# Transposing k one chunk earlier, with its sums of squares on TensorE, and shorter stated waits behind two triangular solves

## The chip, the cores and the metric

The kernel runs on one core of a Trainium2 chip. Its measure is the time of one execution on the device, in microseconds (us). The engines are PE (matrix products), DVE (vector), ACT (activations), POOL (the second vector engine) and SP (which issues the DMAs spoken of here). Each engine takes its instructions in the order of the program.

## The reference, cut to what matters

The reference is a block with attention, pooling and a mixture of experts, followed by a second block of two layers. Only the second block's layers are changed. One of them projects the 512 tokens onto many columns and feeds three branches, whose outputs are gated and projected back. The branch that the change touches is a gated delta rule:

```
h = rms_norm_2(x, norm_g[layer])
cols = split_columns(h @ w_in[layer])
...
qkv = jax.nn.silu(centred_depthwise_conv(qkv, conv_w))
q, k, v = jnp.split(qkv, [GDN_QK_W, 2 * GDN_QK_W], axis=-1)
...
k = l2_normalize(k.reshape(b, l, GDN_HEADS, GDN_DK))
...
a_mat = beta[..., :, None] * jnp.einsum('nhcid,nhcjd->nhcij', k, k) * d_strict
...
sol = lax.linalg.triangular_solve(a_mat, rhs, left_side=True, lower=True, unit_diagonal=True)
...
_, o = lax.scan(step, s0, xs)
```

`l2_normalize` multiplies by the reciprocal root of the sum of squares over a head's 64 columns. The second branch is a latent attention (`mla_branch`), the third a recurrence (`rwkv7_branch`) that the kernel also evaluates in chunks with a triangular solve of its own.

## The kernel before, in words

The first block takes the first 838 us. Each layer of the second block then goes through the same stages, layer 0 from about 838 to 1395 us and layer 1 from there to the end.

The projection (`Project`) makes 27 chunks of 128 columns. A chunk is eight steps of three products `mm<-hh,wh`, `mm<-hl,wh`, `mm<-hh,wl`; three such products are called a triple here, so a chunk is 8 triples. The plan of chunks is: the decay inputs, the three of k, four of the gate, three of q, three of v, seven of the third branch's, two of the attention's latents, four of the gate. Behind a chunk of q, k or v, `qkv` (L1281) convolves it along the tokens with one ACT and four DVE instructions (L1289, L1293), applies silu with a tanh on ACT and a product on DVE (L1296, L1303), and puts a function `take` on a list, with the count of chunks after which `columns` (L1223) calls it. `take_k` (L1427) transposes k into the tile `kt` (PE L159, ACT L1432).

`Gdn` then works in this order: `gates` and `triangles` (decay factors); `keys` (L1500) squares `kt` on POOL, sums the squares on DVE, normalizes `kt` (L1515) and transposes it back into `kq`; `squares` (L1549, tiles `x<-kq`) makes the products of keys and multiplies them into the triangle `M`; `inverse` (L1608) sends `M` through DRAM (`mud`) into the tile `au`, one triangle to a partition, and `solve` (L1332) inverts blocks of 32 x 32 by 30 steps of two dependent DVE instructions each (`stmp<-au`, `au<-au,stmp`). The result goes through DRAM (`xud`) to the tile `XT`, is transposed by DVE (L1633, L1635) and completed to 64 x 64 by PE (`x<-XT,AO`, then `x<-LT,XT`, from `off_diagonal`). `chain` (L1646) carries the state over eight steps (`kp`, `pu`, `kp`) and ends in four output groups (`kp`, `pu` of 24 products each).

`Rwkv.prepare` (L1804) is the third branch's preparation: its products `mm<-w,rw`, `mm<-cst,lw`, `mm<-cst,sq` depend on one another through DVE; then come triangles (`x<-KR,BB`, `M`), the same kind of solve, and `mm<-XT,AO`, followed by its states. The attention `mla` (L2149) has products `mm<-mch,...`, `mm<-kT,qT`, `mm<-cst,e` and `mo`.

The order of PE is written by hand. Each stage is a generator; `yield x` says that the stage's next PE work should wait until x us of PE work, by the kernel's own count `pe_us`, has been issued from elsewhere. `braid` (L161) takes the first stream that is due, so the number sets how much other work stands between two pieces of a stage; it is no wait on the chip. Streams are woven as `first` (gates to inverse) with `project`, `second` (the chain) with `project`, then `project`, which goes on into `prepare`, with `others` (attention, then rows of the output projection), then `states` with `others`. A stage whose input is late holds PE, since everything behind it is queued. The other engines' orders come from a scheduler and are fixed too. The lines of the waits in question:

```
        yield 19
        for t in range(NT):
...
        yield 44
        while not self.decayed:
...
        yield 26
        yield from off_diagonal(net, lambda: self.pa.tile([128, 2, 512], F32, name="x2", bufs=1), self.AO, XP, LT, T, 24, fac)
...
                yield 50
                yield from off_diagonal(net, lambda: psum.tile([128, 1, 512], F32, name="mm", bufs=2), AO, XP, LT, T, 16, None)
```

Of the kernel before, what the change touches and what calls it, by code (L numbers as in the profile page):

```python
# [8 lines left out]
F32 = mybir.dt.float32  # L9
# [3 lines left out]
AF = mybir.ActivationFunctionType  # L13
ALU = mybir.AluOpType
AX = mybir.AxisListType
PSUM = bass.MemoryType.PSUM

S = 512
D = 1024
NT = 4  # L20
# [78 lines left out]
def tok(t):  # L99
    return slice(128 * t, 128 * t + 128)  # L100
# [1027 lines left out]
class Project:  # L1128
# [152 lines left out]
    def qkv(self, g, ms):  # L1281


        net, nc, tmp = self.net, self.net.nc, self.tmp
        cw = net.smalls.cw[:, self.l]
        for m in ms:
            ps = yield from self.columns()
            y = tmp.tile([128, S], F32, name="y", bufs=4)
            nc.scalar.activation(y, ps, AF.Copy, scale=cw[:, 2, m:m + 1])  # L1289
            for j in (0, 1, 3, 4):  # L1290
                d = j - 2
# [5 lines left out]
            if m < 3:  # L1297
                z = g.kq[:, m, :, 64:128]
# [5 lines left out]
            self.pend.append((self.count + 1, partial(self.take, g, m, y)))  # L1304

    def take(self, g, m, y):
        (g.take_q, g.take_k, g.take_v)[m // 3](self, m % 3, y)
        g.have.add(m)
# [72 lines left out]
class Gdn:  # L1381


    def __init__(self, net, ctx, a, l, ab):
        self.net, self.a, self.l = net, a, l
        tc, nc = net.tc, net.nc
        p = self.pool = ctx.enter_context(pool(tc, "gd"))
# [23 lines left out]
        m = self.midp = self.mid.enter_context(pool(tc, "gdm"))  # L1411
# [5 lines left out]
        self.kt = self.ta.tile([128, NT, 384], F32, name="kt", bufs=1)  # L1417

# [8 lines left out]
    def take_k(self, pj, m, z):  # L1427
        net, nc = self.net, self.net.nc
        ps = pj.psum.tile([128, 512], F32, name="tr", bufs=1)
        for t in range(NT):  # L1430
            net.transpose(ps[:, tok(t)], z[:, tok(t)], net.ident)
        nc.scalar.activation(self.kt[:, :, tok(m)], ps.rearrange("p (t c) -> p t c", t=NT), AF.Copy)  # L1432
# [67 lines left out]
    def keys(self):  # L1500

        net, nc, tmp, psum, kt = self.net, self.net.nc, self.ta, self.pa, self.kt
        while not self.have.issuperset((3, 4, 5)):
            yield 1
        ss = tmp.tile([128, NT, 6], F32, name="ss", bufs=1)
        for t in range(NT):
            sq = tmp.tile([128, 6, 64], F32, name="sq", bufs=1)
            kv = kt[:, t].rearrange("p (h d) -> p h d", d=64)
            nc.gpsimd.tensor_tensor(sq, kv, kv, op=ALU.mult)
            nc.vector.tensor_reduce(ss[:, t], sq, AX.X, ALU.add)  # L1510
        r = net.rstd(tmp, ss.rearrange("p t h -> p (t h)"), [128, 24], 1, 1e-6, "rk").rearrange("p (t h) -> p t h", t=NT)
        yield 19
# [95 lines left out]
    def inverse(self, mud, xud):  # L1608
# [14 lines left out]
        yield 44  # L1623
# [16 lines left out]
        yield 26  # L1640
# [108 lines left out]
class Rwkv:  # L1749
# [54 lines left out]
    def prepare(self, mud, xud):  # L1804
# [16 lines left out]
        with pool(tc, "rka", 1, "right") as tmp, pool(tc, "rks", 2, "right") as small, pool(tc, "rpa", 1, "right", PSUM) as psum:  # L1821
# [160 lines left out]
            def inverse():  # L1982
# [24 lines left out]
                yield 50  # L2007
# [531 lines left out]
```

## Time and profile before

| | |
|---|---|
| three runs | 1902.6, 1907.91 (median), 1915.12 us |
| profiled execution | 1903.25 us, span 1901.5 us |
| mean granted clock of PE | 0.930 of full speed |
| PE busy | 1653.5 us (87%), 14010 instructions |
| DVE busy | 1046.3 us (55%) |
| ACT, POOL busy | 583.7 us (31%), 558.4 us (29%) |

The span runs from the first to the last instruction of the profiled execution; 1.75 us of its time lie around it. Busy shares are means over stages with different limits: in one stage PE never pauses, in another it waits for a result from DVE or from DRAM. A wait is shown with the engine and line that ended it; "issue" is idle time that ended with nothing that the profile shows. A granted clock of 1.0 is 2.4 GHz, one near 0.5 is 1.2 GHz.

### The profile page before, as it was taken

To read this page: it belongs to the slowest core of one execution; us is meant where nothing else is said; L and a number is where in the kernel's file an instruction comes from. 1 tells how busy PE (TensorE), PEld (TensorE's weight loads), DVE (VectorE), ACT (ScalarE), POOL (GpSimd) and SP (SyncE) were. 2 spreads that over 40 slices of the span, in tenths; PEclk is the share of its full clock that TensorE was granted. 3 is DMA by queue.
4 is the path that set the end of the run, shared out by engine and by line. 5 is a ranking of instruction groups with operands and counts; after the bars stand their busy time and mean duration, and the time that the engine had idled before them with its cause. 6 is when DMAs were issued, how large, how long until landed. Compare 5 with 4: busy or idle time off the path is not lost.

```text
span 1901.5 us, 34119 instructions
## 1 busy us (share of the span) xinstructions
PE 1653.5 (87%) x14010; PEld 1100.7 (58%) x14010; DVE 1046.3 (55%) x2224; ACT 583.7 (31%) x1154; POOL 558.4 (29%) x559
## 2 busy tenths in 40 slices
PE   5999998999999999959978968777789799789776
PEld 3986584444444444438756755455577577545554
DVE  2435534344434333355895567836656875678456
ACT  4344432212121212144432124331344331244212
POOL 1113111000000000025651243454335721354443
PEclk8899998999999999979988989898889999989888
DMA  9934726999999999833424120123433441201332
GB/s 310 238 107 139 257 74 221 393 392 398 399 406 400 392 399 396 308 102 95 106 68 99 62 73 21 30 93 106 133 84 94 112 111 50 53 33 39 99 111 89
DMA packets 243219, 337.10 MB, mean 177 GB/s; under 512 B 92769, under 2 KB 166161, under 8 KB 226225
## 3 DMA queue, kind: packets, MB, share of 16 engines
q1 hardware_dynamic: 241152, 329.88, 50.3%
q10 hardware_dynamic: 1152, 3.22, 0.5%
q8 instruction: 112, 1.84, 0.4%
q0 software_dynamic: 752, 1.76, 0.3%
q14 instruction: 51, 0.41, 0.1%
HBM read 310.84 MB, written 23.99 MB: 176 GB/s over the span
## 4 chain that ended last, share of the span: by engine, by line
PE 25%; DVE 17%; DMA 5%; issue 4%; POOL 3%; ACT 2%; SPq 1%; DVEq 0%; POOLq 0%; ACTq 0%
PE mm L149 17%; DVE stmp L1342 2%; DVE au L1344 2%; PE mm L159 2%; PE tr L149 1%; PE x L149 1%; PE pu L149 1%; PE kp L149 1%; DMA w<-in_w_out_dram 1%; DMA au<-mud 1%; DVE nm L2233 1%; DVE y L1293 1%; PE mo L149 1%; DMA gate<-gated 1%; POOL w L2310 1%
## 5 line engine op out<-in xcount | busy, mean ns | idle before, releaser
L149 PE MATMUL gu<-w,XT 128*64 128x512 f32 x1024 | 225.8, 594 | 0.0
L149 PE MATMUL mm<-hh,wh 128*128 128x512 f32 (+1 forms) x464 | 203.9, 440 | 0.0
L149 PE MATMUL mm<-hh,wl 128*128 128x512 f32 (+1 forms) x464 | 188.4, 406 | 0.0
L149 PE MATMUL mm<-hl,wh 128*128 128x512 f32 (+1 forms) x464 | 188.1, 405 | 0.0
L928 POOL TENSOR_TENSOR yl<-y,yh 128x512 fp32r<-128x512 f32 x30 | 38.1, 1270 | 451.4 <-ACT yh L927 451.4
L149 PEld LDWEIGHTS gu<-w,XT 128*64 128x64 f32 x1024 | 72.1, 137 | 142.7 <-issue 136.2
L938 DVE TENSOR_TENSOR xres<-mm,xres 128x512 f32<-128x512 f32 x128 | 79.2, 681 | 90.7 <-PE mm L149 90.7
L149 PE MATMUL mm<-w,hT 128*64 128x512 f32 x512 | 113.4, 595 | 0.7 <-ACT hT L912 0.7
L149 PE MATMUL mm<-w,mh 128*128 128x512 f32 x256 | 92.9, 442 | 22.8 <-POOL w L2310 10.0
L149 PEld LDWEIGHTS mm<-hh,wh 128*128 128x128 f32 (+1 forms) x464 | 91.6, 198 | 26.6 <-issue 3.5
L149 PEld LDWEIGHTS mm<-hh,wl 128*128 128x128 f32 (+1 forms) x464 | 91.1, 196 | 21.0
L149 PEld LDWEIGHTS mm<-hl,wh 128*128 128x128 f32 (+1 forms) x464 | 91.8, 198 | 19.1 <-DVE hl L1162 0.2
L1214 ACT ACTIVATE wh<-w 128x1024 fp32r<-128x1024 f32 (+1 forms) x54 | 57.0, 1056 | 145.8 <-PE mm L149 105.9
L1216 POOL TENSOR_TENSOR wl<-w,wh 128x1024 fp32r<-128x1024 f32 (+1 forms) x28 | 69.4, 2478 | 110.0 <-ACT wh L1214 91.3
L149 PE MATMUL mm<-wh,hh 128*128 128x256 f32 x320 | 93.8, 293 | 2.2 <-ACT hh L357 2.2
L149 PE MATMUL mm<-wh,hl 128*128 128x256 f32 x320 | 91.0, 284 | 4.3 <-DVE hl L359 4.0
L2238 POOL TENSOR_SCALAR e<-e,rs 128x512 f32<-128x512 f32 x48 | 75.5, 1574 | 65.3 <-DVE rs L2237 59.8
L149 PE MATMUL mm<-wl,hh 128*128 128x256 f32 x320 | 90.6, 283 | 1.6 <-DVE wl L381 1.6
L149 PEld LDWEIGHTS mm<-w,hT 128*64 128x64 f32 x512 | 35.3, 137 | 66.6 <-issue 62.5
L149 PEld LDWEIGHTS mm<-w,mh 128*128 128x128 f32 x256 | 50.1, 206 | 41.1 <-POOL w L2310 12.5
L1342 DVE TENSOR_TENSOR stmp<-au 96x60 f32<-96x60 f32 (+29 forms) x120 | 64.5, 537 | 14.3 <-DMA au<-rmud 6.5
L872 ACT ACTIVATE X<-mm,ws 128x512 f32<-128x512 f32 x32 | 22.0, 688 | 151.4 <-DVE ws L869 128.1
(580 smaller groups left out, 3596.3 us busy)
## 6 DMA issues: line engine op xcount, KB each, us to landing
w<-in_w_gate_dram SPq DMA_DIRECT2D x64, 1024.0 KB, 13.2
w<-in_w_up_dram SPq DMA_DIRECT2D x64, 1024.0 KB, 13.4
w<-in_w_down_dram SPq DMA_DIRECT2D x64, 1024.0 KB, 10.0
w<-in_w_in_dram SPq DMA_DIRECT2D x52, 512.0 KB, 4.1
w<-in_w_ada_dram SPq DMA_DIRECT2D x24, 1024.0 KB, 8.5
w<-in_w_out_dram SPq DMA_DIRECT2D x16, 512.0 KB, 3.8
w<-in_w_in_dram SPq DMA_DIRECT2D x6, 1024.0 KB, 12.1
w<-in_w_out_dram SPq DMA_DIRECT2D x4, 1024.0 KB, 6.3
```

What stands on the lines that cost most here:

```text
L149: return self.nc.tensor.matmul(out, a, b, **kw)
L159: return self.nc.tensor.transpose(out, a, ident)
L872: nc.scalar.activation(X[:, 512 * i:512 * i + 512], ps, AF.Copy, scale=ws[:, 1:2])
L928: (nc.vector if last else nc.gpsimd).tensor_tensor(yl[:, hs], y, yh[:, hs].bitcast(F32), op=ALU.subtract)
L938: nc.vector.tensor_tensor(net.xres[:, t, hs], po, net.xres[:, t, hs], op=ALU.add)
L1214: nc.scalar.activation(h[:, :, :m], w[:, :, :m], AF.Copy)
L1216: eng.tensor_tensor(lo[:, :, :m], w[:, :, :m], h[:, :, :m].bitcast(F32), op=ALU.subtract)
L1293: nc.vector.scalar_tensor_tensor(y[:, lo:hi], ps[:, lo + d:hi + d], cw[:, j, m:m + 1], y[:, lo:hi], op0=ALU.mult, op1=ALU.add)
L1342: nc.vector.tensor_tensor(tv, au[:n, :, j + 1:, j:j + 1].to_broadcast(sh), au[:n, :, j:j + 1, 0:j].to_broadcast(sh), op=ALU.mult)
L1344: nc.vector.tensor_tensor(au[:n, :, j + 1:, 0:j], au[:n, :, j + 1:, 0:j], tv, op=ALU.add)
L2233: nc.vector.tensor_reduce(nm, ps, AX.X, ALU.max, negate=True)
L2238: nc.gpsimd.tensor_scalar(e, e, rs, None, op0=ALU.mult)
```

## The change

`qkv` makes, for a chunk of k, a second tile `sq` with the squares of the convolved k, by one ACT instruction more, and puts `take_k` on the list for the end of the next chunk in place of the one after that. `take_k` first multiplies the squares by a constant of 128 x 2 (`head`), four PE instructions `tr<-cst,sq`, which sums them over each head, copies the sums by DVE to a new tile `kss`, and then transposes as before. `keys` loses its four POOL squares and four DVE sums, and its stated wait goes from 19 to 8. Three more stated waits change: in `inverse` 44 to 34 and 26 to 20, in `Rwkv.prepare`'s `inverse` 50 to 42.

```diff
@@ -1301,10 +1301,15 @@
                 nc.scalar.activation(c8(y), z, AF.Square)
             else:
                 nc.vector.scalar_tensor_tensor(y, th, 1.0, y, op0=ALU.add, op1=ALU.mult)
-            self.pend.append((self.count + 1, partial(self.take, g, m, y)))
-
-    def take(self, g, m, y):
-        (g.take_q, g.take_k, g.take_v)[m // 3](self, m % 3, y)
+            if m // 3 == 1:
+                sq = tmp.tile([128, S], F32, name="sq", tag="y", bufs=4)
+                nc.scalar.activation(sq, y, AF.Square)
+                self.pend.append((self.count, partial(self.take, g, m, y, sq)))
+            else:
+                self.pend.append((self.count + 1, partial(self.take, g, m, y)))
+
+    def take(self, g, m, *y):
+        (g.take_q, g.take_k, g.take_v)[m // 3](self, m % 3, *y)
         g.have.add(m)
 
     def rw(self, rw):
@@ -1415,6 +1420,7 @@
         self.ta = self.sa.enter_context(pool(tc, "gda", 2))
         self.pa = self.sa.enter_context(pool(tc, "gpa", 1, "left", PSUM))
         self.kt = self.ta.tile([128, NT, 384], F32, name="kt", bufs=1)
+        self.kss = self.ta.tile([128, NT, 6], F32, name="kss", bufs=1)
 
 
     def take_q(self, pj, m, z):
@@ -1424,8 +1430,12 @@
             net.matmul(ps[:, 2 * t:2 * t + 2], z[:, tok(t)], net.const("head"), start=True, stop=True)
         nc.vector.tensor_copy(self.ssq[:, :, :, m], ps[:, :8].rearrange("p (t a) -> p t a", t=NT))
 
-    def take_k(self, pj, m, z):
+    def take_k(self, pj, m, z, sq):
         net, nc = self.net, self.net.nc
+        ps = self.pa.tile([128, 512], F32, name="tr", bufs=2)
+        for t in range(NT):
+            net.matmul(ps[:, 2 * t:2 * t + 2], sq[:, tok(t)], net.const("head"), start=True, stop=True)
+        nc.vector.tensor_copy(self.kss[:, :, 2 * m:2 * m + 2], ps[:, :8].rearrange("p (t a) -> p t a", t=NT))
         ps = pj.psum.tile([128, 512], F32, name="tr", bufs=1)
         for t in range(NT):
             net.transpose(ps[:, tok(t)], z[:, tok(t)], net.ident)
@@ -1502,14 +1512,8 @@
         net, nc, tmp, psum, kt = self.net, self.net.nc, self.ta, self.pa, self.kt
         while not self.have.issuperset((3, 4, 5)):
             yield 1
-        ss = tmp.tile([128, NT, 6], F32, name="ss", bufs=1)
-        for t in range(NT):
-            sq = tmp.tile([128, 6, 64], F32, name="sq", bufs=1)
-            kv = kt[:, t].rearrange("p (h d) -> p h d", d=64)
-            nc.gpsimd.tensor_tensor(sq, kv, kv, op=ALU.mult)
-            nc.vector.tensor_reduce(ss[:, t], sq, AX.X, ALU.add)
-        r = net.rstd(tmp, ss.rearrange("p t h -> p (t h)"), [128, 24], 1, 1e-6, "rk").rearrange("p (t h) -> p t h", t=NT)
-        yield 19
+        r = net.rstd(tmp, self.kss.rearrange("p t h -> p (t h)"), [128, 24], 1, 1e-6, "rk").rearrange("p (t h) -> p t h", t=NT)
+        yield 8
         for t in range(NT):
             kv = kt[:, t].rearrange("p (h d) -> p h d", d=64)
             nc.vector.tensor_tensor(kv, kv, r[:, t, :, None].to_broadcast([128, 6, 64]), op=ALU.mult)
@@ -1620,7 +1624,7 @@
         nc.sync.dma_start(xud, au)
         for z in range(2):
             nc.sync.dma_start(XP[half(z)], xud[48 * z:48 * z + 24].rearrange("u b i c -> (b i) u c"))
-        yield 44
+        yield 34
         while not self.decayed:
             yield 1
         LT = self.LT = self.pool.tile([128, 2, 24, 64], F32, name="LT", tag="ld")
@@ -1637,7 +1641,7 @@
         nc.vector.tensor_scalar(fac, bu[:, 0], -1.0, None, op0=ALU.mult)
         for b in (0, 2):
             nc.vector.memset(fac[quarter(b)], -1.0)
-        yield 26
+        yield 20
         yield from off_diagonal(net, lambda: self.pa.tile([128, 2, 512], F32, name="x2", bufs=1), self.AO, XP, LT, T, 24, fac)
 
         yield 2
@@ -2004,7 +2008,7 @@
                     nc.vector.transpose(LT[quarter(b), 0, :, c0:c0 + 32], XP[quarter(b)])
                     if b % 2:
                         nc.vector.transpose(XP[quarter(b)], LT[quarter(b), 1, :, c0:c0 + 32])
-                yield 50
+                yield 42
                 yield from off_diagonal(net, lambda: psum.tile([128, 1, 512], F32, name="mm", bufs=2), AO, XP, LT, T, 16, None)
 
             def rest():
```

Lines from `qkv` on stand five to ten lines lower in the changed kernel. Counted in triples since the layer's first transposes of `mch`, both layers alike, PE's order has k's transposes behind triples 24, 32 and 40 before and 16, 24 and 32 now; the last product of `squares` behind 82 before and 57 now; `x<-XT,AO` behind 174 before and 133 now. Between the last of `squares` and `x<-XT,AO` stand 92 triples before and 76 now. The chain's eight steps and four output groups began behind 175 and ran on into `prepare`, which begins behind 208; now they lie between 140 and 188. Between the last product of the third branch's triangles and its `mm<-XT,AO` stand 18 products `mm<-kT,qT`, 60 `mm<-cst,e`, 48 `mo`, 4 `mm<-wv,mch` and one `mm<-t,cst` before, and 13, 52, 56, none and none now. From a layer's start to that `mm<-XT,AO` the order now holds 2 `mm<-kT,qT`, 8 `mm<-cst,e` and 16 `mo` more than before, which stood behind it.

PE at the start of `Rwkv.prepare` in layer 0, before. The products with `w`, `lw` and `sq` are `prepare`'s; `kp` and `pu` are the chain's, and the products of 24 begin its output groups:

```order
L149 MATMUL mm<-rw,w_7715 128x512
L149 MATMUL pu<-rhs,LT 64x64 x12
L149 MATMUL mm<-cst,lw 128x128 x4
L149 MATMUL kp<-VS,KD 64x64 x12
L149 MATMUL mm<-cst,lw 128x128 x4
L149 MATMUL kp<-SA,kq 64x64 x12
L159 MATMUL mm<-cst,sq 128x128 x4
L149 MATMUL pu<-rhs,LT 64x64 x12
L159 MATMUL mm<-cst,s_9967 128x128 x4
L149 MATMUL kp<-SA,kq 64x64 x24
L149 MATMUL pu<-VS,LT 64x64 x24
L149 MATMUL mm<-rw,w_7715 128x512
```

The same place in the changed kernel, where `mch` is the attention's input, and `wk`, `wn`, `wr` its weights:

```order
L149 MATMUL mm<-w_7716,rw 128x256 x4
L149 MATMUL mm<-rw,w_7716 128x512
L149 MATMUL mm<-cst,lw 128x128 x4
L149 MATMUL mm<-mch,cst 32x512
L149 MATMUL mm<-cst,lw 128x128 x4
L149 MATMUL mm<-mch,wk 128x512
L149 MATMUL mm<-mch,wn 128x512 x2
L159 MATMUL mm<-cst,sq 128x128 x4
L149 MATMUL mm<-mch,wk 128x512
L149 MATMUL mm<-mch,wn 128x512 x2
L159 MATMUL mm<-cst,s_10319 128x128 x4
L149 MATMUL mm<-mch,wk 128x512
```

The chain's steps are gone from between the products of `prepare`, and the attention's stand there.

DVE within the solve in layer 0, before. The rows of `stmp` and `au` are the solve's; `y` is a convolution, `DT` a decay factor's:

```order
L1344 TENSOR_TENSOR au<-au,stmp 96x2x25x6
L1293 SCALAR_TENSOR_TENSOR y<-mm,smalls,y 128x510
L1342 TENSOR_TENSOR stmp<-au 96x336
L1293 SCALAR_TENSOR_TENSOR y<-mm,smalls,y 128x511
L1344 TENSOR_TENSOR au<-au,stmp 96x2x24x7
L1293 SCALAR_TENSOR_TENSOR y<-mm,smalls,y 128x511
L1342 TENSOR_TENSOR stmp<-au 96x368
L1293 SCALAR_TENSOR_TENSOR y<-mm,smalls,y 128x510
L1344 TENSOR_TENSOR au<-au,stmp 96x2x23x8
L1342 TENSOR_TENSOR stmp<-au 96x396
L1303 SCALAR_TENSOR_TENSOR y<-th,y 128x512
L1344 TENSOR_TENSOR au<-au,stmp 96x2x22x9
```

DVE in the solve in the changed kernel, from the same step on (`kq<-th,y` is the silu of a chunk of q, `ssq` a copy of its sums):

```order
L1347 TENSOR_TENSOR stmp<-au 96x300
L1349 TENSOR_TENSOR au<-au,stmp 96x2x25x6
L1431 COPY ssq<-tr 128x8
L1216 TENSOR_TENSOR wl<-w,wh 128x1024
L1347 TENSOR_TENSOR stmp<-au 96x336
L1293 SCALAR_TENSOR_TENSOR y<-mm,smalls,y 128x510
L1349 TENSOR_TENSOR au<-au,stmp 96x2x24x7
L1293 SCALAR_TENSOR_TENSOR y<-mm,smalls,y 128x511
L1347 TENSOR_TENSOR stmp<-au 96x368
L1293 SCALAR_TENSOR_TENSOR y<-mm,smalls,y 128x511
L1349 TENSOR_TENSOR au<-au,stmp 96x2x23x8
L1293 SCALAR_TENSOR_TENSOR y<-mm,smalls,y 128x510
```

The convolutions that now stand between the solve's rows are q's and v's. Over the whole solve DVE has, in both layers, 20 convolution rows now where it had 7, five rows of silu where it had 2, three copies `ssq` where it had none, the same four rows `DT`, three rows `wl<-w,wh` where it had 2 in layer 0 and 3 in layer 1, and four rows `rw` of the third branch's inputs where it had 6 and 8, besides one and two `kx`.

## Rows read from the trace of the kernel before

**Rows 1.** Windows: length, busy PE, PEld, DVE, ACT, POOL (instructions), PEclk, DMA share, GB/s.

```profile
838.00:1395.00 557.00, 454.64 (x4938) 335.57 (x4938) 363.84 (x687) 183.75 (x344) 232.58 (x237) 0.89 0.29 81
...
1395.00:1901.00 506.00, 423.71 (x4826) 312.45 (x4826) 338.38 (x662) 163.20 (x314) 225.24 (x230) 0.91 0.28 79
...
945.00:1004.00 59.00, 45.10 (x269) 35.25 (x268) 56.16 (x84) 21.12 (x34) 30.80 (x30) 0.91 0.25 75
...
1091.00:1130.50 39.50, 28.88 (x780) 23.36 (x779) 28.00 (x58) 9.94 (x20) 15.06 (x18) 0.95 0.25 64
...
1130.00:1150.00 20.00, 15.32 (x89) 7.48 (x89) 14.15 (x27) 5.57 (x12) 13.47 (x16) 0.57 0.24 78
...
1624.00:1660.00 36.00, 28.17 (x780) 22.68 (x778) 25.21 (x43) 9.44 (x19) 15.13 (x18) 0.95 0.21 58
```

**Rows 2.** Waits of PE, 856 to 1032: releaser, us in total, times, longest.

```profile
PE tr L159 <- ACT rw L1317: 4.2, 1, 4.2
```

**Rows 3.** Waits of PE, 1131 to 1240, first layer.

```profile
PE mm L159 <- POOL e L2238: 10.2, 2, 7.4
...
PE mm L149 <- DVE lw L1834: 4.2, 1, 4.2
```

**Rows 4.** Waits of PE, 1624 to 1770, second layer.

```profile
PE mm L149 <- DVE lw L1834: 7.3, 1, 7.3
...
PE mm L149 <- DVE XT L2006: 4.6, 2, 2.5
...
PE mm L159 <- POOL e L2238: 3.0, 2, 2.7
```

**Rows 5.** Timeline of PE, first layer: start, length, engine, line, operation, tiles, [idle].

```profile
873.32 0.39 PE L149 MATMUL mm<-hh,wh 128*128 128x512 f32 x1
...
874.00 0.39 PE L149 MATMUL mm<-hh,wh 128*128 128x512 f32 x1
...
874.68 0.60 PE L159 MATMUL tr<-cst,y 128*128 128x128 f32 x4
...
923.02 0.95 PE L149 MATMUL tr<-cst,y 128*128 128x2 f32 x8
...
926.15 0.74 PE L149 MATMUL x<-kq 64*64 64x64 f32 x24
...
1031.92 1.82 PE L149 MATMUL x<-XT,AO 32*32 32x32 f32 x192
```

**Rows 6.** Timeline of PE, second layer.

```profile
1465.39 0.74 PE L149 MATMUL x<-kq 64*64 64x64 f32 x24
...
1564.23 1.54 PE L149 MATMUL x<-XT,AO 32*32 32x32 f32 x159
...
1568.63 0.66 PE L149 MATMUL x<-XT,AO 32*32 32x32 f32 x33 [2.86 <-issue]
```

**Rows 7.** Timeline of ACT behind k's first chunk.

```profile
869.92 0.63 ACT L1296 ACTIVATE th<-y 128x512 f32<-128x512 f32 x1
...
870.45 1.04 ACT L1214 ACTIVATE wh<-w 128x1024 fp32r<-128x1024 f32 x1
```

**Rows 8.** Timeline of DVE in the solve and behind it, both layers.

```profile
956.69 0.73 DVE L1293 SCALAR_TENSOR_TENSOR y<-mm,smalls,y 128x510 f32<-128x510 f32 x1
...
957.35 0.89 DVE L1342 TENSOR_TENSOR stmp<-au 96x336 f32<-96x336 f32 x1
...
1016.42 0.97 DVE L1635 STREAM_TRANSPOSE XT<-LT 32x768 f32<-32x768 f32 x1
...
1560.19 0.97 DVE L1635 STREAM_TRANSPOSE XT<-LT 32x768 f32<-32x768 f32 x1
```

**Rows 9.** Timeline of DVE and PE, the second branch's solved blocks, first layer.

```profile
1233.69 0.71 DVE L2006 STREAM_TRANSPOSE XT<-LT 32x512 f32<-32x512 f32 x1
...
1243.27 1.29 PE L149 MATMUL mm<-XT,AO 32*32 32x32 f32 x128
```

**Rows 10.** Groups of PE, 1182 to 1243: operation, tiles, shape, count | busy us, mean ns.

```profile
L149 PE MATMUL mm<-kT,qT 96*128 96x512 f32 x36 | 20.3, 656 | 0.0
```

## The prediction

> **What bounds the kernel now.** I read the busy times by stage first. In both layers that the change touches PE works some four fifths of the time: 454.64 of 557 us in layer 0 and 423.71 of 506 in layer 1 [rows 1]. So PE's own work and its idle pieces make the time, and since the change takes almost nothing off PE, the question is which idle pieces go and which come. The waits of PE by releaser come next, stage by stage: the reader is to see that no single wait is large, that layer 0 has one of 4.2 us before the blocks' products [rows 2], and that most of the rest sits behind the solves, on DVE and POOL rows [rows 3, 4]. Then two windows over the chain's last steps and its output groups: 39.5 us with 28.88 busy in layer 0, 36 with 28.17 in layer 1 [rows 1]. That is 10.6 and 7.8 us idle, where the chain had run out of projection to stand beside. Last the timelines, for the path from the keys to the solved blocks: DVE is busy for 56.16 of 59 us while it solves [rows 1], so there the solve is limited by DVE, and any row put between its steps lengthens it.
>
> **The change part by part.**
>
> The sums of squares. Three times in a layer PE gets four small products. The trace has the same form for q, 0.95 us for a group of four [rows 5], so six groups cost 5.7 us. The DVE sums and POOL squares that go lay beside a busy PE, and PE did not wait for them; I count them at nothing. The shorter stated wait of 8 gives the normalization that follows 14 triples (46 less 32), 14 by 0.68 us from the distance of two equal products [rows 5], or 9.5 us; I see no wait there. If that cover failed by some us, it would be again in the range.
>
> The first chunk of k. Its products with the squares are due at the end of the next chunk: eight triples, 5.5 us, ahead of the transposes at 874.68, hence at 869.2 [rows 5]. The square comes behind the tanh (869.92, 0.63 us), DVE's product and the conversion `wh`, which ends at 871.49 [rows 7]. Another ACT pass of the size of that tanh ends at 872.1. PE is held for 2.9 us in each layer: 5.8 us. Zero would need ACT to run earlier than now, 5 would need a second conversion in front; the later two chunks have no table to load, so I add nothing for them.
>
> The waits ahead of the blocks' products. The 4.2 us of layer 0 [rows 2] belong to a chunk of the third branch that now stands behind `x<-XT,AO`, and 2.86 us of layer 1 [rows 6] are a gap within those products, which a longer wait just before would absorb. Gain: 7.1 us.
>
> The wait for the solved blocks. From the end of `squares` to the last transposed block the trace has 1017.4 less 926.9, 90.5 us, in layer 0 and 1561.2 less 1466.1, 95.1 us, in layer 1; to PE's arrival at `x<-XT,AO` it has 105.0 and 98.1 us [rows 5, 6, 8]. So PE came late by 14.5 and 3.0 us. Now 16 triples fewer stand there, 10.9 us, and in layer 0 the 4.2 us go as well: PE comes after 89.9 and 87.2 us. If the solve takes as long as before, the new wait is 0.6 and 7.9 us. But DVE now has 13 more convolutions between the solve's steps, 0.66 us each from one row's start to the next [rows 8], or 8.6 us; the other rows of the exchange nearly cancel. With all of that the waits are 9.2 and 16.5 us. The bounds are therefore 8.5 and 25.7 us together. As some of these rows may fit while the solve waits for POOL, I take the middle, 17.1 us.
>
> The chain. It begins 35 triples earlier in PE's order and so has projections beside all eight steps. The 10.6 and 7.8 us idle should shrink; but the output groups now have one triple between them, and the chain's steps depend on DVE. Ends: nothing and 18.4 us. I take half, 9.2.
>
> The third branch's preparation. The waits for `lw`, 4.2 us and 7.3 us [rows 3, 4], stood between products that depend on one another through DVE, with the chain between them. Now the attention's products stand there. Ends again nothing and 11.5; half is 5.7 us gained.
>
> The third branch's solved blocks. Its solve is not changed. Ahead of `mm<-XT,AO` five products `mm<-kT,qT` fewer stand, 20.3 us for 18 products of two records each [rows 10], so 1.13 us each and 5.6 us in all, and with the smaller ones about 7. In layer 0 the blocks were ready at 1234.4 and PE came at 1243.3 [rows 9]; without 7 us of work, and without half of the 7.4 us that it waited for POOL's `e` [rows 3], it comes at 1232.6 and waits 1.8 us: 1.9 us gained, and the same if the whole of `e` goes. In layer 1 PE already waited 4.6 us for `XT` [rows 4], so 7 us less cover are 7 us more wait. Together 5.1 us lost (0 to 12).
>
> The sum. 5.7 + 5.8 - 7.1 + 17.1 - 9.2 - 5.7 + 5.1 = 11.7 us longer. On the profiled execution's 1903.25 us that gives 1915 us. That execution is 0.2% below the median of the three runs, so against the median it is 0.4%, less than the 1% that a measurement of this kernel can tell from no change.
>
> **A rule on the clock.** Behind 2.5 and 4.2 us of waiting, the trace shows the granted clock at 0.57 from 1130 to 1150, about the lower of its two levels (1.2 GHz), with PE busy 15.32 us; at the 0.95 of the window before it, the same work takes 9.2, so the stretch cost 6.1 us [rows 1, 3]. The sum leaves this out, since it takes two such stretches to go (behind `lw`) and two to come (behind `x<-XT,AO`). The Trainium skill, "TensorE: Matmul & The Clock Gate", section "Why this matters for your kernels", asks for no idle gaps between bursts, since the clock falls back to half behind them. The trace agrees with 0.57. By that rule the two new waits cost their stretches for certain, and the two old ones only go if the waits for `lw` go.
>
> **The rivals.**
>
> Half clock twice more. The new waits bring their stretches, and the old ones stay, as a wait of 2 or 3.6 us is left at `lw`. For it: the 0.57. Against it: the first wait may be only some us long in layer 0. 11.7 + 2 x 6.1 gives 23.9, 1927 us.
>
> DVE is the bound (slower). All 13 convolutions lengthen the solve (25.7 in place of 17.1 us), and the waits in the chain and for `lw`, all of them ended by DVE rows, stay as long as they are, whatever stands beside them. For it: 56.16 of 59 us, and that every large wait but `e` is on DVE. Against it: in the chain's window DVE is busy for 28.00 of 39.5 us only [rows 1]. 11.7 + 8.6 + 9.2 + 5.7 = 35.2 gives 1938 us. It decides from the point where DVE has no pause left in the solve.
>
> The cover pays (faster). The solve keeps its length, because DVE takes the convolutions while the solve waits; the new waits are 8.5 us; the chain's idle time and the waits for `lw` go wholly, and with them the two slow stretches. 11.7 - 8.6 - 9.2 - 5.8 - 12.2 = -24.1 gives 1879 us. For it: the windows of the chain are idle by a quarter. Against it: DVE had only 2.8 us of pause in the solve.
>
> Nothing moves on balance. The order permutes the same work and each wait is followed by a shorter one: 1903 to 1908 us.
>
> **How the numbers follow.** The forecast has 0.40, with a range of its own from 1902 to 1928 by the ends of the waits; half clock 0.10, DVE the bound 0.20, the cover 0.19, nothing 0.11. From 1881 to 1940 some 0.1 is left out below and some 0.1 above. One per cent is 19 us: slower by more than that are DVE's case almost whole (0.19), most of half clock (0.07) and the upper end of the forecast (0.08), 0.34; faster is the cover's case but for its edge, 0.17; within 1% remains 0.49.
>
> **What would show it.** A wait of PE for a square on ACT of about 3 us at the first `tr<-cst,sq` of each layer; a wait of 1 to 9 us at `x<-XT,AO` in layer 0 and of 8 to 17 in layer 1, ended by DVE's transposes; the solve's rows spread over more than 59 us; the chain's steps without idle time before the layer's last projections; at `mm<-XT,AO` of layer 1 a wait of some 12 us. The wait for `rw` of 4.2 us should be missing. The forecast is wrong if the solve is as short as before, if the products of `prepare` wait for each other more than now, or if the clock stays down for long behind `x<-XT,AO`.

## The result and the profile after

| | before | changed |
|---|---|---|
| median of 8 runs each | 1908.18 us | 1925.55 us |
| lowest to highest | 1902.6 to 1915.12 us | 1914.3 to 1933.64 us |
| ratio, 95% interval | | 1.009 (1.0069 to 1.0112) |
| profiled execution | 1903.25 us, span 1901.5 | 1933.54 us, span 1931.7 |
| mean granted clock | 0.930 | 0.912 |

The change costs 0.9%, some 17 us, where 0.4% was forecast. The changed kernel's profiled execution is one of its slowest, 8 us above its median, and that of the kernel before lies 5 us below its own, so the rows below show more loss (30 us) than the runs do on the mean; verdicts below rest on the ratios.

The first view is that of windows over the two layers, from the first transposes of `mch` to the last product of the layer. The columns are those of [rows 1]. Before:

```profile
856.20:1395.40 539.20, 439.77 (x4882) 324.42 (x4882) 355.52 (x676) 171.91 (x327) 227.69 (x233) 0.90 0.29 81
...
1395.40:1893.80 498.40, 423.70 (x4826) 312.45 (x4826) 334.34 (x655) 161.90 (x310) 224.59 (x229) 0.91 0.28 78
```

After, with three shorter windows behind the two layers:

```profile
859.70:1396.40 536.70, 449.07 (x4907) 330.86 (x4907) 355.28 (x675) 173.76 (x330) 226.54 (x229) 0.89 0.29 81
...
1396.40:1924.10 527.70, 449.33 (x4850) 326.98 (x4850) 335.68 (x654) 164.46 (x313) 218.60 (x225) 0.87 0.26 74
...
1009.00:1023.00 14.00, 6.10 (x199) 5.19 (x200) 8.02 (x9) 0.63 (x1) 0.00 (x0) 0.51 0.50 94
...
1029.00:1109.00 80.00, 75.18 (x1178) 58.90 (x1178) 44.45 (x101) 15.16 (x21) 19.07 (x22) 0.96 0.23 66
...
1699.00:1719.00 20.00, 20.00 (x244) 10.57 (x239) 9.43 (x19) 6.17 (x15) 3.42 (x6) 0.50 0.01 2
```

The reader is to take busy PE from the length. Layer 0 was idle for 99.4 us and is for 87.6; layer 1 for 74.7 and 78.4. So PE waits 8 us less in both layers together than before, and still the span is 30 us longer. It is the busy time that rose, by 9.3 and 25.6 us, and only 6 us of that are new products (the 24 records of `tr<-cst,sq` of 128x2 take 3.0 us in each layer). The rest is the same products taking longer. The groups of the same shape and count in layer 1 show it, before:

```profile
L149 PE MATMUL mm<-hh,wh 128*128 128x512 f32 x208 | 90.8, 437 | 0.0
...
L149 PE MATMUL mm<-kT,qT 96*128 96x512 f32 x48 | 25.0, 608 | 0.0
```

and after:

```profile
L149 PE MATMUL mm<-hh,wh 128*128 128x512 f32 x208 | 93.9, 452 | 0.0
...
L149 PE MATMUL mm<-kT,qT 96*128 96x512 f32 x48 | 30.1, 722 | 0.0
```

The 48 records of the attention's scores took 25.0 us and now 30.1, the 208 of one projection product 90.8 and 93.9.

The waits of PE in the changed kernel, from 856 to 1032 and from 1131 to 1264 us in layer 0, are

```profile
PE x L149 <- DVE XT L1639: 6.2, 2, 5.5
...
PE x L149 <- DMA XT<-xud: 4.5, 1, 4.5
...
PE tr L149 <- ACT y L1301: 3.0, 1, 3.0
...
PE tr L149 <- ACT sq L1306: 2.7, 1, 2.7
...
PE mm L149 <- DVE SC L1951: 6.2, 3, 4.4
...
PE mm L149 <- DVE XT L2010: 4.9, 2, 3.0
...
PE mm L159 <- POOL e L2242: 0.8, 2, 0.6
```

and in layer 1, from 1400 to 1565 and from 1656 to 1812 us,

```profile
PE x L149 <- DVE XT L1639: 6.3, 2, 5.6
...
PE tr L149 <- ACT y L1301: 5.7, 1, 5.7
...
PE tr L149 <- ACT sq L1306: 2.7, 1, 2.7
...
PE x L149 <- DMA XT<-xud: 2.2, 1, 2.2
...
PE mm L149 <- DVE SC L1951: 5.9, 1, 5.9
...
PE mm L149 <- DVE XT L2010: 5.1, 2, 2.9
...
PE mm L149 <- DVE lw L1838: 1.3, 2, 0.7
```

In the kernel before, from 856 to 1032 us in layer 0 and from 1395 to 1572 in layer 1, a wait for the tile `rh` (ahead of a group `x<-kq`) stood besides that of [rows 2]:

```profile
PE x L149 <- ACT rh L1602: 5.8, 1, 5.8
...
PE x L149 <- ACT rh L1602: 5.2, 1, 5.2
```

In the changed kernel the waits for `rh` on ACT are gone, the wait for `rw` of [rows 2] is gone, those for `e` of [rows 3, 4] are next to nothing or not in the list and those for `lw` of [rows 3, 4] fell from 4.2 and 7.3 to 1.3 in each layer. In their place stand waits at the first branch's blocks (`XT`, L1639 and the DMA: 10.7 and 8.5 us), one for the first square, one for `y`, the squares of a chunk of q, of 3.0 and 5.7 us, and a longer one for `SC` (a product of `x` and a mask that DVE makes for the third branch; its waits were 1.9 us in layer 0 before).

### The profile page after: what moved, and what is told of

It is laid out like the page before. It is cut to its first block, busy times and chain, and to the rows that moved or that the text cites. A ratio compares the mean times of both kernels' runs of the same rounds, so it can differ in the third digit from the quotient of the medians.

```text
span 1931.7 us, 34211 instructions
## 1 busy us (share of the span) xinstructions
PE 1692.3 (88%) x14058; PEld 1126.9 (58%) x14058; DVE 1047.4 (54%) x2222; ACT 588.3 (30%) x1160; POOL 550.5 (28%) x551
## 5 line engine op out<-in xcount | busy, mean ns | idle before, releaser
L149 PE MATMUL mm<-hh,wh 128*128 128x512 f32 (+1 forms) x464 | 208.7, 450 | 0.0
## 6 DMA issues: line engine op xcount, KB each, us to landing
w<-in_w_gate_dram SPq DMA_DIRECT2D x64, 1024.0 KB, 13.2
w<-in_w_in_dram SPq DMA_DIRECT2D x6, 1024.0 KB, 12.2
```

What stands on the lines that cost most here:

```text
L149: return self.nc.tensor.matmul(out, a, b, **kw)
```

## The experiments

The theories, in the order in which they were taken up: too little cover ahead of the solved blocks (1); work at the lower clock (2); the k part itself (3); the chain's new place (4); the earlier take (5). Each kernel was run beside the kernel before on the same chip, and the ratio decides. Idle and busy are PE's in both layers together, by the windows of one profiled execution each, as above. These executions lie off their kernels' medians by up to 10 us: that of the kernel before 5 us below, the changed kernel's 8 above, e2's 6 above, e8's 6, e6's 9 and f3's 10 below. A difference of some us in the last two columns is therefore within their scatter.

| kernel | ratio to before (95%) | median, us | idle, us | busy, us |
|---|---|---|---|---|
| before | | 1908.18 | 174.1 | 863.5 |
| changed | 1.009 (1.0069 to 1.0112) | 1925.55 | 166.0 | 898.4 |
| e1: k part, waits 44, 26, 50 | 1.0108 (1.0054 to 1.0162) | 1927.91 | 164.7 | 894.8 |
| e2: waits alone | 1.0066 (1.0047 to 1.0086) | 1918.38 | 172.4 | 882.3 |
| e3: changed, 44 and 26 back | 1.0105 (1.0069 to 1.0141) | 1925.11 | 163.0 | 892.9 |
| e4: changed, 50 back | 1.0158 (1.0098 to 1.0218) | 1933.03 | 172.3 | 893.9 |
| e5: k part, chain back | 1.0251 (1.022 to 1.0282) | 1951.98 | 182.0 | 901.6 |
| e6: changed, fill at the blocks | 1.0066 (1.004 to 1.0092) | 1917.99 | 149.3 | 893.4 |
| e7: before, fill at mix | 1.006 (1.0037 to 1.0082) | 1915.88 | 164.2 | 887.9 |
| e8: changed, two chunks again | 1.0086 (1.0053 to 1.012) | 1919.07 | 164.0 | 883.1 |
| e11: changed, five fills | 1.0239 (1.0192 to 1.0285) | 1951.1 | 146.5 | 939.1 |
| f1: sums on TensorE alone | 1.0017 (0.9999 to 1.0035) | 1911.61 | 161.7 | 884.5 |
| f2: early take alone | 1.0045 (1.0026 to 1.0064) | 1915.36 | 171.6 | 876.3 |
| f3: third branch's wait alone | 0.9941 (0.992 to 0.9961) | 1894.89 | 165.5 | 854.5 |

**e1, the k part alone.**

```diff
-        yield 34
+        yield 44
...
-        yield 20
+        yield 26
...
-                yield 42
+                yield 50
```

> k's squares and transposes as in the changed kernel, with the four-number part undone: the three stated waits at the solved blocks are 44, 26 and 50 again. Between the last of squares and the blocks' products PE then has 95 triples (92 before, 76 changed). Theory 1 (too little cover ahead of the solved blocks): waits at the first branch's XT,AO under 3 us per layer, at the third branch's under 4, time 1900 to 1912 us, equal to before or a little faster, since the chain now ends behind triple 203 and is covered. Theory 2 (the clock: the same idle time, but more work at the lower clock behind longer waits): the mean granted clock returns to 0.925 to 0.935 as the waits go, and PE's busy time falls by 15 us or more against the changed kernel. Theory 3 (the k part itself costs): 1918 us or more, with waits for the squares and the silu of k and q of some 6 us per layer.

Measured: 1.0108, as slow as the whole change. Its layers by the windows:

```profile
858.40:1404.50 546.10, 455.56 (x4907) 336.82 (x4907) 355.57 (x675) 174.01 (x330) 224.82 (x229) 0.88 0.28 80
...
1404.50:1917.90 513.40, 439.21 (x4850) 322.86 (x4850) 334.11 (x654) 163.87 (x314) 218.31 (x225) 0.89 0.27 76
```

Idle is 9 us less than before, busy 31 more. Theory 1, that the cover ahead of the solved blocks is what costs, falls: the waits at the blocks are gone here (2 us of "issue" at most) and nothing came back. The clock did not return either (0.917). Theory 3 had named both the time and the waits: PE waits 2.7 us for the first square in each layer and 4.2 and 3.1 us for `y`, the squares of a chunk of q. Its times for e3, e4 and e5 below came out too, but not that for e2, where the k part is missing and the time rose all the same.

**e2, the waits alone**, in the kernel before.

```diff
-        yield 44
+        yield 34
...
-        yield 26
+        yield 20
...
-                yield 50
+                yield 42
```

> The kernel before with nothing but the three stated waits changed to 34, 20 and 42. Between the last of squares and the blocks' products stand 71 triples. Theory 1: PE waits some 10 us per layer at XT,AO and as long as in the changed kernel at the third branch's blocks, time 1916 to 1930 us. Theory 2: the same, with a mean granted clock of 0.91 to 0.92. Theory 3: within 5 us of before, 1903 to 1913 us.

Measured: 1.0066, 1918.38 us, with 172.4 us idle (174.1 before) and 19 us more busy, clock 0.912. The time lies in the range of theories 1 and 2, but again idle time does not make it.

**e3 and e4, one group of waits back each**, in the changed kernel.

```diff
# e3
-        yield 34
+        yield 44
...
-        yield 20
+        yield 26
# e4
-                yield 42
+                yield 50
```

> The changed kernel with the two stated waits of the first branch's solve back at 44 and 26, and 42 kept for the third branch. Theory 1: the waits of 10.7 and 8.5 us at XT,AO go, those of some 5 us at the third branch's blocks stay, time 1907 to 1917 us. Theory 2: more than these waits is won, as the work behind XT,AO runs at the full clock: 1903 to 1910 us. Theory 3: 1918 us or more.

> The changed kernel with the third branch's stated wait back at 50 and the first branch's kept at 34 and 20. Theory 1: the waits at the third branch's blocks (4.9 and 5.1 us) shrink by the four scores products of cover that come back, 4 to 5 us per layer, and those at XT,AO stay: 1915 to 1921 us. Theory 2: the same or a little more. Theory 3: 1920 us or more.

Measured: 1.0105 for e3, within the interval of the changed kernel, where theories 1 and 2 had both wanted a gain; 1.0158 for e4, by its median slower than the changed kernel, though the two intervals overlap. Theories 1 and 2 had wanted a gain there; theory 3 names no more than a lower bound, and it is kept. So the longer stated wait for the third branch, meant as cover, won nothing and probably cost.

**e5, the k part with the chain in its old place.**

```diff
-        yield 34
+        yield 60
...
-        yield 20
+        yield 26
...
-                yield 42
+                yield 50
```

> k's part as in the changed kernel, with stated waits of 60, 26 and 50, so that the first branch's chain stands again where it stood before: XT,AO behind triple 173 (174 before), the chain from 176 and, as before, on into the third branch's preparation; 16 scores products ahead of the third branch's blocks, as before. Theory 4 (what costs is that the chain no longer stands between the products of the third branch's preparation, so that more of PE's order runs in short bursts and pauses at the lower clock): 1900 to 1911 us, PE's working time at the lower clock back to some 140 to 155 us in both layers together. Theory 3 (the k part itself costs, its 5 us of products and 3 us waits for squares and what follows): 1915 us or more. Theory 1 (cover ahead of the blocks) expects 1900 to 1912 too, but was already contradicted by the run with the old waits.

Measured: 1.0251, the slowest of all. Theory 4, that the loss is the chain's absence from the third branch's preparation, falls with it: PE's order from the chain on is nearly that of before, and the loss is the largest.

```profile
860.70:1407.30 546.60, 452.61 (x4907) 332.62 (x4907) 360.20 (x675) 174.56 (x330) 226.18 (x229) 0.88 0.28 80
...
1407.30:1944.30 537.00, 449.00 (x4850) 329.81 (x4850) 339.29 (x654) 164.36 (x314) 216.56 (x225) 0.87 0.26 72
```

Idle is 8 us more than before, busy 38 more, of which 6 are products. Layer 1 holds most of it.

**e6, unread products ahead of the blocks**, and **e7, the same in the kernel before, ahead of mix.** A helper issues products that nothing reads.

```diff
+    def spin(self, ps, n):
+        for _ in range(n):
+            self.nc.tensor.matmul(ps, self.ident, self.c[:, :512], start=True, stop=True)
...
# e6
+        net.spin(self.pa.tile([128, 512], F32, name="tr", bufs=2), 10)
         yield from off_diagonal(net, lambda: self.pa
# e7
         yield 0.5
+        if self.mix is not None and n == 3:
+            net.spin(psum.tile([128, 512], F32, name="tr", bufs=2), 10)
         turn(0)
```

> The changed kernel with ten products of 128 x 512, whose results nobody reads, ahead of the first branch's XT,AO in each layer. They fill the wait of some 10 us there and so keep PE at work; they take no time from anything if the wait is as long as they are. Theory 2 (time is lost as work at the lower clock): the stretch of low clock behind the wait goes, 1914 to 1922 us. If only idle time counted: 1925 to 1931 us, unchanged or longer.

> The kernel before with ten such unread products in each layer ahead of the transposes of mix, where PE waits 9.7 and 8.0 us for a DMA and the clock is low from 1280 to 1301 and from 1803 to 1823. Theory 2: the low stretches there shrink and 4 to 10 us are won, 1896 to 1902 us beside 1906. If only idle time counted: 1904 to 1912 us.

e6 measured 1.0066 and 1917.99 us, in the range of theory 2; its interval overlaps that of the changed kernel, so a gain of some 0.2% is possible, not certain. What is plain is the clock at the place itself:

```profile
1006.82 8.75 PE L160 MATMUL tr<-cst 128*128 128x512 f32 x20
...
1015.50 0.26 PE L149 MATMUL x<-XT,AO 32*32 32x32 f32 x6
```

Twenty records of fill took 8.75 us, the blocks followed at once, and the window there is

```profile
1005.00:1019.00 14.00, 12.95 (x222) 7.21 (x221) 9.42 (x11) 0.83 (x2) 0.00 (x0) 1.00 0.53 101
```

Where the changed kernel had a granted clock of 0.51 from 1009 to 1023, this one has 1.00 from 1005 to 1019. e7 is a miss of theory 2: the fill took the place of the wait for `mix` in the same way and the mean clock of the runs rose (0.930, beside 0.925 for the kernel before), but the time rose too, by 0.6%. Idle fell by 10 us, while two fills of 20 records, 10.7 and 9.5 us long here, were added.

**e8, two chunks again**, in the changed kernel, and **e11, fill in five waits.**

```diff
# e8
-                self.pend.append((self.count, partial(self.take, g, m, y, sq)))
+                self.pend.append((self.count + 1, partial(self.take, g, m, y, sq)))
# e11, beside e6
+        if m == 0:
+            net.spin(ps, 3)
...
+        if m == 0:
+            net.spin(ps, 4)
...
+                    if d == 1 and t == 1:
+                        net.spin(pv, 5)
...
+    if fac is None:
+        net.spin(pt[:, 0], 8)
```

> The changed kernel with k's products and transposes two chunks behind again, and all else of the change kept (squares summed on TensorE, all four stated waits). The wait of 2.7 us for the first square in each layer goes, and the squares of keys come 8 triples later (behind 65). Theory 5 (the early take is what hurts, by its wait and the low clock behind it): 1908 to 1916 us. Theory 2 (low clock behind the waits further on, at the blocks and in the third branch's preparation, whichever part made them): 1918 to 1928 us, within 4 us of the changed kernel less the 5.4 us of the two waits at most.

> The changed kernel with unread products in five waits of each layer: ten ahead of the first branch's XT,AO as in the run before, and besides three ahead of the first product with k's squares, four ahead of the first of q's, five ahead of the product that waits for SC (4.4 and 5.9 us), eight ahead of the third branch's XT,AO. Theory 2: the low clock goes with them, the shortfall of the clock (one less the granted clock, times the span) falls below 130 us (170 in the changed kernel, 137 with the fill at the blocks alone), and the time to 1905 to 1915 us, below the 1918 of the fill at the blocks alone. If the waits alone counted, the products would only cost where they are longer than the waits: 1920 to 1930 us.

e8 measured 1.0086, the changed kernel's ratio: within the change, the earlier take is not what costs. e11 measured 1.0239 with a clock of 0.924, so a shortfall of 148 us, and 1951 us, against every expectation. Its fill is 26 us of work in each layer, 53 in all, and idle fell by 20 only against the changed kernel: the products filled the waits that they stood in front of, and other waits grew behind them. In e7 and e11 work that is not needed took longer than what the clock gave back.

**f1, f2 and f3, one edit alone each**, in the kernel before.

```diff
# f1: the change's qkv, take_k and keys, with
-                self.pend.append((self.count, partial(self.take, g, m, y, sq)))
+                self.pend.append((self.count + 1, partial(self.take, g, m, y, sq)))
...
-        yield 8
+        yield 19
...
# f2
-            self.pend.append((self.count + 1, partial(self.take, g, m, y)))
+            self.pend.append((self.count + (m // 3 != 1), partial(self.take, g, m, y)))
# f3
-                yield 50
+                yield 42
```

In f1 the three other stated waits are those of before.

> The kernel before with nothing but the source of k's sums of squares changed: ACT squares, TensorE products, DVE copies in place of POOL squares and DVE sums; transposes two chunks behind, all stated waits as before (19, 44, 26, 50). PE's order is that of before with three groups of four small products more in each layer. If the products count by their own length: 1905 to 1912 us (5 us more than before). If the k part loses by the low clock whatever its place (as the runs with the k part and the old chain suggest): 1920 us or more, with a shortfall of the clock of 150 us or more (133 before).

> The kernel before with k's transposes one chunk behind in place of two, and nothing else: POOL squares, DVE sums and all stated waits as before. Squares of keys end behind triple 77 (82 before), XT,AO stands behind 169. If the early take loses by a short wait for the silu of k's first chunk and the low clock behind it: 1908 to 1918 us. If it is free: 1900 to 1908 us.

> The kernel before with the third branch's stated wait at 42 and nothing else: four scores products and what goes with them less ahead of its blocks. If the cover counts: waits of 9 us in layer 1 at the third branch's XT,AO (4.6 before) and of a few in layer 0, 1909 to 1916 us. If the low clock decides and the products now stand beside the states: 1898 to 1908 us.

f1 measured 1.0017, 3 us and by its interval at most 7, no more than its products take: the sums on TensorE are not the trouble by themselves. f2 measured 1.0045: the earlier take alone costs some 9 us, though it adds no work. f3 measured 0.9941, 11 us faster than before and the fastest kernel of all. By the table it has 9 us less idle and 9 us less busy than before, at the same work; its profiled execution is its fastest, so some of that is scatter. The wait at the third branch's blocks in layer 1 did grow as cover went, to 5.53 + 2.47 + 1.90 = 9.9 us (4.6 before, [rows 4]):

```profile
1744.06 0.31 PE L149 MATMUL mm<-XT,AO 32*32 32x32 f32 x2 [5.53 <-DMA XT<-rxud]
...
1746.84 0.32 PE L149 MATMUL mm<-XT,AO 32*32 32x32 f32 x4 [2.47 <-DVE XT L2006]
...
1749.06 1.91 PE L149 MATMUL mm<-XT,AO 32*32 32x32 f32 x122 [1.90 <-DVE XT L2006]
```

and the four scores products that no longer stand ahead of the blocks stand behind them, beside the states. The layers' idle time fell all the same, and it fell there. From the last group of `mm<-XT,AO` to the layer's end, layer 0 and layer 1, before:

```profile
1243.27:1395.40 152.13, 110.65 (x1405) 81.86 (x1404) 85.34 (x155) 40.65 (x77) 61.50 (x62) 0.85 0.36 113
...
1766.51:1893.80 127.29, 99.49 (x1342) 73.04 (x1342) 64.51 (x132) 29.06 (x56) 53.18 (x56) 0.86 0.28 94
```

and in f3:

```profile
1230.31:1381.80 151.49, 116.46 (x1447) 86.94 (x1445) 91.61 (x162) 44.43 (x85) 67.15 (x65) 0.86 0.36 113
...
1749.06:1875.70 126.64, 101.94 (x1382) 75.99 (x1382) 71.23 (x140) 34.40 (x69) 58.43 (x59) 0.88 0.29 97
```

The products moved there add 8 us of busy time, and the stretches are no longer than before: idle is 9.6 us less in these two executions.

## Why the prediction was right or wrong, point by point

**The path to the blocks: right in its mechanism, not in each size.** The rows of the changed kernel on it:

```profile
913.76 0.74 PE L149 MATMUL x<-kq 64*64 64x64 f32 x24
...
1010.67 0.31 PE L149 MATMUL x<-XT,AO 32*32 32x32 f32 x2 [4.50 <-DMA XT<-xud]
...
1016.52 0.31 PE L149 MATMUL x<-XT,AO 32*32 32x32 f32 x4 [5.54 <-DVE XT L1639]
...
1692.14 1.09 PE L159 MATMUL mm<-cst,sq 128*128 128x128 f32 x4 [1.72 <-DVE sq L1880]
...
1693.02 1.91 PE L149 MATMUL mm<-t,cst 96*96 96x512 f32 x2
...
1694.72 1.18 PE L149 MATMUL mm<-wv,mch 128*128 128x384 f32 x2
...
1698.21 0.63 PE L159 MATMUL mm<-cst,s 128*128 128x128 f32 x4 [2.30 <-DVE s L1880]
...
1698.77 1.97 PE L149 MATMUL x<-KR,BB 64*64 64x64 f32 x64
```

From the last of `squares`, which ended at 914.5, PE came to the blocks at 1010.67 less the wait of 4.50, after 91.7 us (forecast 89.9), and waited 10.7 us there in three pieces, the last of 0.7, which is above the forecast's bounds (0.6 to 9.2). In layer 1 it waited 8.5, near the lower bound (7.9 to 16.5), because it came there after 92.7 us and not after 87.2; on the way the wait for `rh` had gone and that for q's `y` had come, and the sum has neither. The two waits add up to 19.2 us, and that the term of 17.1 is so near is in part luck. The view of the solve's tile shows why, with the first and last start of its 30 products (stmp) in layer 0 and layer 1. Before:

```profile
L1342 DVE TENSOR_TENSOR stmp<-au x30: 218/643/2139, 946.5 to 1002.2; 96x60 f32<-96x60 f32 x2, 96x116 f32<-96x116 f32 x2, 96x168 f32<-96x168 f32 x2, 96x216 f32<-96x216 f32 x2
...
L1342 DVE TENSOR_TENSOR stmp<-au x30: 210/636/2012, 1485.4 to 1543.6; 96x60 f32<-96x60 f32 x2, 96x116 f32<-96x116 f32 x2, 96x168 f32<-96x168 f32 x2, 96x216 f32<-96x216 f32 x2
```

and after:

```profile
L1347 DVE TENSOR_TENSOR stmp<-au x30: 218/629/2322, 934.7 to 1002.7; 96x60 f32<-96x60 f32 x2, 96x116 f32<-96x116 f32 x2, 96x168 f32<-96x168 f32 x2, 96x216 f32<-96x216 f32 x2
...
L1347 DVE TENSOR_TENSOR stmp<-au x30: 218/630/2499, 1471.6 to 1539.0; 96x60 f32<-96x60 f32 x2, 96x116 f32<-96x116 f32 x2, 96x168 f32<-96x168 f32 x2, 96x216 f32<-96x216 f32 x2
```

They span 68.0 us for 55.7 in layer 0 and 67.4 for 58.2 in layer 1. The 13 convolutions were priced at 8.6 us in each, and the bound that takes them whole was the nearer one; 12.3 and 9.2 were added.

**The squares: right.** PE waited 2.7 us for the first square in each layer (forecast 2.9), and f1 prices the products at 3 us for both layers (0 to 7 by its interval) in place of 5.7.

**Chain and preparation: right in direction.** The window of the chain from 1029 to 1109 has 75.18 of 80 us busy, where a quarter was idle at its end before [rows 1]; the wait for `lw` fell to 1.3 us in each layer. PE's waits on the chain's own rows (`kp`, `pu`) fell from 6.9 to 4.7 us in layer 0 and from 7.4 to 2.7 in layer 1, 6.9 us where the sum took 9.2; those for `lw` by 8.9 us where it took 5.7. Waits of the attention's products, 2.8 us in each layer, came into the preparation.

**The third branch's blocks: the size by luck, the sign wrong.** The sum took 5.1 us lost from less cover, 1.9 gained in layer 0 and 7 lost in layer 1. In the changed kernel PE waits 5.1 us there in each layer, where it waited for nothing in layer 0 and for 4.6 us in layer 1: 5.6 us are lost, but in the layer where a gain was forecast. In f3 the wait did grow in layer 1, from 4.6 to 9.9 us, yet the edit as a whole gains 11 us: the products taken away are not lost as cover, they stand beside later pauses, where 9.6 us of idle time went. The step that failed is "7 us less cover are 7 us more wait": nearly true at the place when the edit stands alone, not for the layer.

**Waits that were not foreseen.** The sum has none of these: `rh` (11.0 us gone in both layers), most of the waits for `e` (13.2 us before and 0.8 now; it counted 3.7 us of them), `y` (8.7 us come) and `SC`. PE waits 4.4 and 5.9 us for `SC`. The rows of layer 0 show the reason:

```profile
1208.75 1.29 PE L149 MATMUL x<-KR,BB 64*64 64x64 f32 x32
...
1210.66 0.20 DVE L1347 TENSOR_TENSOR stmp<-au 128x30 f32<-128x30 f32 x1 [5.85 <-DMA au<-rmud]
...
1216.42 0.75 DVE L1951 TENSOR_TENSOR SC<-x,mk 128x256 f32<-128x256 f32 x2
```

The solve's first step waits 5.85 us for its triangle to come back from DRAM, and `SC` stands behind eight of the solve's products `stmp` in DVE's order. Its input, PE's `x<-KR,BB`, was done at 1210.0; `SC` began 6.4 us later. In the order of before, this `SC` stood among the solve's rows too, in layer 0 behind thirteen of them:

```profile
1202.07 0.75 DVE L1947 TENSOR_TENSOR SC<-x,mk 128x256 f32<-128x256 f32 x2
```

But PE had waited 7.4 us for `e` just ahead [rows 3] and then waited only 0.6 us for `SC`. So in layer 0 the wait for `e` went and one at `SC` came. In layer 1 `SC` moved from behind three of the solve's products to behind ten.

**The clock: the step that failed.** The sum entered it as nothing: "two such stretches to go" and "two to come". Taken together, the terms of the sum other than the 5.7 us of products made 6.0 us more idle time; the profile has 8 less. On the waits alone, the change should have paid. That it is slower, as forecast, and that its time lies within the forecast's range of 1902 to 1928 us, is therefore luck. What it lost is busy time at the lower clock: 35 us more busy in the profiled execution, 6 of them products. In the window from 1699 to 1719 PE is busy for 20.00 of 20 us at a granted clock of 0.50; ahead of it stand, in PE's rows, waits of 1.72 and 2.30 us with short work between. The same stage before, with the same triangles `x<-KR,BB`, had 1.00:

```profile
1695.00:1715.00 20.00, 18.03 (x232) 10.21 (x230) 15.90 (x31) 9.38 (x21) 6.45 (x7) 1.00 0.07 28
```

All runs on record agree. Their mean clock is 0.917 for the changed kernel, and 0.924 to 0.927 for the runs of the kernel before that stand beside e1 to f3. The shortfall (one less the clock, times the span) is 159 us for the one and 139 to 145 us for the other. The difference of 14 to 20 us is about the whole loss of 17; it is an estimate, since the shortfall counts idle time at the lower clock too. The rival "half clock twice more" was right in kind, but its 1927 us came near 1925.55 by luck as well, as it adds 12.2 us of clock to the same 11.7 us. Nor was it right in place: the windows of 20 us in layer 1 have 0.57 in the third branch's preparation (from 1696), 0.69 beside its solve (from 1756) and 0.72 at its blocks (from 1796), where `x<-XT,AO` has 0.76 (from 1536).

**What is shown and what stays open.** Shown by the runs: no one of these alone is the loss: the sums on TensorE (f1), the earlier take within the change (e8), the missing cover at the blocks (e1, e3), the chain's place (e5). The third branch's 42 gains alone (f3), probably also on top of the first branch's 34 and 20 with the k part (e4 against the changed kernel, with intervals that overlap), and nothing beside 44 and 26 (e1 against e3). The first branch's 34 and 20 cost 1.2% on the kernel before with 42 (f3 to e2) and nothing with the k part and 42 (e3 to the changed kernel). So the parts do not add up; the changed kernel is what is left of a gain of 0.6% and losses of one to two. Where the time rose at equal work (e2, f2), busy rose with a lower clock. That the clock is the cause of the 0.9% is still in part argued: with waits filled the clock rose in e6, e7 and e11, and of these only e6 may have gained. One edit was never tried by itself, the shorter stated wait of `keys` (19 to 8). It stands in e1 (1.0108) but not in f1 (1.0017) and f2 (1.0045), so some 0.5% are left to it, or to the parts of the k part together. Not shown, too, is why the k part with the chain in its old place is the slowest; that the waits of one to three us behind which the clock falls lie differently in it is a guess that no run tried.

**A version that beats both:** the kernel before with the third branch's stated wait at 42 and nothing else, 0.9941 (0.992 to 0.9961).

## What to carry to other kernels

Before pricing a wait, sum idle and busy of the engine apart: when a change leaves the work alone and its busy time still rises, look at the granted clock next. A forecast from waits alone can come out with the right sign for the wrong reason, as here. Judge idle and busy from more than one execution, or beside the clock of all runs. Change stated waits one at a time: here four edits that went together hid one that gains 0.6%. Work taken away from in front of one wait is not lost if a later pause can use it: in f3 one wait grew by 5 us and the pauses behind it shrank by almost 10.

## What was not expected of the hardware

The lower level of the clock (1.2 GHz) held from 1699 to 1719 while PE was busy without a pause, and it came behind waits of only 1.7 and 2.3 us; elsewhere a wait of that size left it near its full value, as in the chain's window from 1029 to 1109, at 0.96 with a wait of 2.4 us in it. A kernel whose order of PE from the chain on is nearly that of before was 2.5% slower, and repeatably: e5's runs lie between 1946.75 and 1957.1 us, at clocks of 0.910 to 0.916.
